# A hybrid decoder layer on one core: another opening, another order of the leading pieces, x transposes a step later, an end by token tile

## The chip, the core and the metric

The kernel runs on one core of one Trainium2 chip. The metric is the device time of one execution in microseconds. TensorE (PE) multiplies; VectorE (DVE), ScalarE (ACT) and GpSimd (POOL) do the rest, and SyncE (SP) issues most of the transfers. All data is float32.

## The reference

One layer for 256 tokens of width 2048, with float32 weights. Every product with a weight matrix is to be done at near float32 precision.

```python
h = x + 0.5 * swiglu(rmsnorm(h, ffn1_norm), w_gu1, w_dn1)     # d_ff 5632
proj = rmsnorm(h, mix_norm) @ w_in                            # u | v | z | x | B | C | dt
gu, gv, z, xbc, dt_raw = split(proj)
a_out = gelu(gu) * (W_s rmsnorm(gelu(gv)) + b)                # causal inside 128 tokens
m_out = rmsnorm((ssd_scan(silu(conv(xbc)), softplus(dt_raw + bias), ...) + D * x) * silu(z))
h = h + concat([a_out, m_out]) @ w_out
h = h + memory_cross_attention(rmsnorm(h, xa_norm), rmsnorm(mem, mem_norm), w_q, w_kv, w_o)
h = h + 0.5 * swiglu(rmsnorm(h, ffn2_norm), w_gu2, w_dn2)
return rmsnorm(h, final_norm)
```

## The kernel before

**The product.** A float32 operand is split into a rounded part `hi` (a cast on ACT, L143) and a remainder `lo` (a subtraction on DVE, L148). A product is three PE matmuls: hi by hi, hi by lo, lo by hi. All matmuls come from line 73 and all transposes from line 76, and PE runs them in program order.

**The feed-forward steps.** Line numbers here are those of before. `ffn` (used twice) works in columns `c` of 512 gates and 512 ups. A column's product over the 2048 rows of the weight is `proj_sum`: eight *units*, one for each *piece* of 256 rows. A unit loads 1 MB of weights into `raw` (three buffers `wraw`), casts (`whigh`, three buffers), subtracts (`wlow`, two buffers) and multiplies. Of kind C it takes 24 matmuls of 128x512; of kind S (a Strassen-like scheme on sums and differences) 21. The string `GU_KINDS = "CSCSCSCC"` gives each piece its kind. The operand made from the normalised input, `xp_ffn`, has one form per piece: PE transposes four 128x128 tiles of `h` (`tpose`), then for a C piece ACT scales each half of the piece, k = 0 and 1 (L299) and DVE takes the remainder (L300); for an S piece ACT writes `forms` (L352), DVE makes differences (L356 to L358), and ACT and DVE split 3 and 4 forms (L360, L361) into a tile of seven forms. The root-mean-square factor is applied at a column's end, so its sums (`sum_sq`, L273) come beside the first units.

**Steps.** After each unit `step()` counts one and runs the jobs that `later(fn, by)` has put off by that many units. A job's PE transposes therefore stand between two units. The order on DVE, ACT and POOL is set by a scheduler, and each engine runs its row of instructions strictly in that order: an instruction that waits holds up those behind it.

**The opening.** `h` is loaded from `x` by 512 columns and token tile, 256 KB each, and the first three weight pieces by blocks of 256 KB between them, all on SP's queue. `FIRST = [0, 2, 4, 1, 6, 3, 5, 7]` is the order of pieces in the first column of the first step. In the second step the first column runs in plain order.

**The mix stage.** `proj_feat` makes the columns B, C and x of the input projection, feature on the partition, four units a column; `conv_silu` (L530 to L534) convolves them and writes `xf` with ACT, and the job `x_tokens` turns `xf` back to tokens (4 transposes and 2 copies, L637) one unit later for the first half of a column and two for the second. `make_dt` (L562) makes the scan's step sizes with four small matmuls. The x columns are followed by V (the gate's other input), and under it run the scan's first DVE steps `xdt`, `y`, `dec` (L659 to L675) and `gate_weights`.

**The end.** In the last column group `finish(n)` is called for each 512 columns of the output after both token tiles: sums of squares, the factor `rstd_f` (POOL, L281), the scaling and eight output transfers, all on SP's queue (L928).

## Time and profile before

| | us |
|---|---|
| three runs, median (2544.72 to 2545.55) | 2544.92 |
| the profiled execution | 2544.5 |
| its span, from the first to the last instruction | 2542.8 |
| PE busy in it | 2491.5 |
| DVE busy | 1822.0 |
| ACT busy | 1233.8 |
| mean granted clock of PE | 0.993 |

The profiled execution is 0.4 us under the median, and 1.7 us of it lie outside of the span. A row of the timeline gives the start of an instruction, counted from the span's start, its length, and in brackets how long its engine had been idle ahead of it and what ended the wait. Matmuls are pipelined, so the difference of two starts is the cost of one, not its length.

### The profile page before, as it was taken

Reading aid. Unit: us, or ns where it says so; the run is one execution under the profiler, and the core shown is the slowest. Engines: PE = TensorE matmul, PEld = TensorE weight load, DVE = VectorE, ACT = ScalarE, POOL = GpSimd, SP = SyncE. Lnnn points to the kernel's source line nnn. Section 1 sums busy time; section 2 is a strip of 40 time slices with the busy share of each in tenths; the row PEclk is TensorE's granted clock in tenths of the full one; section 3 lists DMA queues with packets and bytes.
Section 4 is the critical chain, followed back from the end, with each engine's and each line's share of the span. In section 5 each row is a group of like instructions: output and inputs, shape, how many; then the busy total and the mean of one; then the engine's idle time right before and its main releaser. Section 6 shows DMA issues by size and latency. Waiting matters only on the chain.

```text
span 2542.8 us, 31168 instructions
## 1 busy us (share of the span) xinstructions
PE 2491.5 (98%) x12732; PEld 2126.1 (84%) x12732; DVE 1822.0 (72%) x1644; ACT 1233.8 (49%) x1100; POOL 21.3 (1%) x44
## 2 busy tenths in 40 slices
PE   7999999999999999999999999999999999999998
PEld 5788888888889997888888999988788888888886
DVE  6888779897776657664555555445689877898886
ACT  5455445555545445434544444334555544555443
POOL 0000000000000000000000000000000000000000
PEclk9999999999999999999999999999999999999999
DMA  5565665656654545555555655555556666666664
GB/s 188 185 208 189 198 211 184 204 193 199 199 173 163 183 151 200 184 166 183 196 184 192 206 182 167 165 169 179 182 184 196 199 198 197 201 198 198 199 208 140
DMA packets 197185, 476.74 MB, mean 187 GB/s; under 512 B 14273, under 2 KB 14433, under 8 KB 196273
## 3 DMA queue, kind: packets, MB, share of 16 engines
q1 hardware_dynamic: 195216, 465.88, 56.2%
q0 software_dynamic: 1680, 8.73, 1.0%
q8 instruction: 99, 1.62, 0.3%
q14 instruction: 46, 0.37, 0.0%
q10 hardware_dynamic: 144, 0.13, 0.0%
HBM read 472.57 MB, written 2.13 MB: 187 GB/s over the span
## 4 chain that ended last, share of the span: by engine, by line
PE 90%; DVE 6%; ACT 2%; issue 1%; DMA 1%; SPq 0%; ACTq 0%; DVEq 0%; POOL 0%
PE acc L73 86%; DVE lo L148 3%; PE tpose L76 2%; ACT hi L143 1%; PE yp L73 1%; DMA raw<-in_w_gu 0%; DVE cacc L532 0%; PE logits L73 0%; PE o L73 0%; DVE sum L159 0%; DVE sum L161 0%; PE mixed L73 0%; DVE sum L160 0%; DVE hids L361 0%; PE dt L73 0%
## 5 line engine op out<-in xcount | busy, mean ns | idle before, releaser
L148 DVE TENSOR_TENSOR lo<-raw,hi 128x2048 fp32r<-128x2048 f32 (+1 forms) x440 | 959.5, 2183 | 443.9 <-PE acc L73 360.0
L143 ACT CAST hi<-raw 128x2048 fp32r<-128x2048 f32 (+1 forms) x440 | 805.1, 1830 | 950.5 <-PE acc L73 802.9
L73 PE MATMUL acc<-hi,xp_ffn 128*128 128x512 f32 x1760 | 558.5, 392 | 10.2 <-ACT xp_ffn L299 6.8
L73 PEld LDWEIGHTS acc<-hi,xp_ffn 128*128 128x128 f32 x1760 | 332.5, 189 | 82.9 <-ACT xp_ffn L299 8.7
L73 PE MATMUL acc<-lo,xp_ffn 128*128 128x512 f32 x880 | 344.4, 391 | 1.2 <-DVE lo L148 1.2
L73 PE MATMUL acc<-hi,hid 128*128 128x512 f32 x1088 | 340.4, 390 | 0.0
L148 DVE TENSOR_TENSOR lo<-sum,hi 128x2048 fp32r<-128x2048 f32 x86 | 196.8, 2289 | 117.3 <-ACT hi L143 117.3
L143 ACT CAST hi<-sum 128x2048 fp32r<-128x2048 f32 x86 | 164.4, 1912 | 178.4 <-DVE sum L161 146.7
L73 PE MATMUL acc<-hi,xt_mix 128*128 128x512 f32 x768 | 244.4, 395 | 0.0
L73 PEld LDWEIGHTS acc<-hi,hid 128*128 128x128 f32 x1088 | 204.2, 188 | 42.3
L73 PE MATMUL acc<-lo,hid 128*128 128x512 f32 x544 | 211.7, 389 | 0.0
L73 PEld LDWEIGHTS acc<-lo,xp_ffn 128*128 128x128 f32 x880 | 166.5, 189 | 36.1 <-DVE lo L148 1.7
L73 PE MATMUL acc<-xt_mix,hi 128*128 128x256 f32 x1024 | 188.5, 286 | 0.0
L73 PEld LDWEIGHTS acc<-hi,xt_mix 128*128 128x128 f32 x768 | 145.5, 189 | 30.8 <-issue 0.7
L73 PEld LDWEIGHTS acc<-xt_mix,hi 128*128 128x128 f32 x1024 | 161.9, 194 | 0.3
L73 PE MATMUL acc<-hi,xp_ffn1s 128*128 128x512 f32 x462 | 150.4, 394 | 3.4 <-ACT hi L143 1.8
L73 PE MATMUL acc<-hi,xp_ffn2s 128*128 128x512 f32 x462 | 150.0, 394 | 3.3 <-DVE xp_ffn L300 2.3
L73 PE MATMUL acc<-lo,xt_mix 128*128 128x512 f32 x384 | 150.6, 392 | 0.0
L73 PE MATMUL acc<-xt_mix,lo 128*128 128x256 f32 x512 | 146.3, 286 | 0.7 <-DVE lo L148 0.7
L408 DVE TENSOR_TENSOR part<-acc,part 128x512 f32<-128x512 f32 x208 | 138.2, 684 | 9.3 <-ACT part L427 4.2
L73 PEld LDWEIGHTS acc<-lo,hid 128*128 128x128 f32 x544 | 102.2, 188 | 20.9
L159 DVE TENSOR_TENSOR sum<-raw 128x1024 f32<-128x1024 f32 x86 | 105.0, 1221 | 7.9 <-DMA raw<-in_w_gu 5.5
(246 smaller groups left out, 3284.1 us busy)
## 6 DMA issues: line engine op xcount, KB each, us to landing
raw<-in_w_gu SPq DMA_DIRECT2D x280, 512.0 KB, 3.9
raw<-in_w_in SPq DMA_DIRECT2D x80, 1024.0 KB, 5.2
raw<-in_w_dn SPq DMA_DIRECT2D x68, 1024.0 KB, 5.5
raw<-in_w_gu SPq DMA_DIRECT2D x144, 256.0 KB, 4.1
raw<-in_w_out SPq DMA_DIRECT2D x32, 1024.0 KB, 5.5
raw<-in_w_kv SPq DMA_DIRECT2D x32, 1024.0 KB, 5.3
raw<-in_w_q SPq DMA_DIRECT2D x16, 1024.0 KB, 5.1
raw<-in_w_o SPq DMA_DIRECT2D x16, 1024.0 KB, 5.5
```

The costliest lines, as they stand in the source:

```text
L73: return pe(nc.tensor.matmul(out, lhsT=lhsT, rhs=rhs, start=start, stop=stop))
L76: return pe(nc.tensor.transpose(out=out, in_=in_, identity=identity))
L143: nc.scalar.copy(out=t[:, :n], in_=x[:, :n])
L148: nc.vector.tensor_tensor(out=t[:, :n], in0=x[:, :n], in1=hi[:, :n].bitcast(F32), op=ALU.subtract)
L159: nc.vector.tensor_tensor(out=t[:, 0:2], in0=raw[:, 0:3:2], in1=raw[:, 3:4].broadcast_to([P, 2, NC]), op=ALU.add)
L408: nc.vector.tensor_tensor(out=out, in0=a, in1=b, op=op)
```

## The change

- **Opening.** `x` is loaded by pieces of 256 columns (both token tiles, 256 KB in rows of 1 KB) in the order in which the pieces are used, between the weight pieces 0, 2 and 4. The first weight piece comes in four blocks of 256 KB, is cast and subtracted by blocks of 512 columns (`split(raw, fine)`), and its unit runs all products of k = 0 ahead of those of k = 1. A new `keep_busy` issues six and then four plain float32 matmuls of 128x256 on zeros (its result is not used), around the transposes of the first piece.
- **Order and kinds of the leading units.** In the first column of both steps the order is `[0, 2, 4, 6, 1, 3, 5, 7]` with kinds `CCCCCSCC`; pieces 1 and 3 have S operands and run as C, with plain forms read from the S operand by `FORM`. For this the S operand holds eight forms rather than seven, and both splits are 128x512 wide.
- **Half steps.** A C unit counts half a step after half of its products and half at its end. The transposes of the pieces are put at half steps, and the sums of squares later.
- **`evac`** is called for each token tile and output half as it ends, no longer for both halves at once.
- **`make_dt`**: the four small matmuls run back to back, and the two DVE steps after them.
- **`x_tokens`** one unit later.
- **The second step's opening**: pieces 4, 6, 5 and 7 are put at 1, 1.5, 2.5 and 3 units, the sums of squares at 3.
- **The end**: `finish(n, t)` is called for each token tile as soon as its columns are done, and two of the eight output transfers go by ACT's queue.

```diff
-    def step(shut=False):
-        steps[0] += 1
+    def step(shut=False, of=1):
+        steps[0] += of
...
+        for b in range(2 * KP):
+            nc.scalar.copy(out=hi[:, b], in_=raw[:, b])
+            nc.vector.tensor_tensor(out=lo[:, b], in0=raw[:, b], in1=hi[:, b].bitcast(F32), op=ALU.subtract)
...
+                def tok(t, k):
+                    if len(x.shape) == 4:
+                        return x[:, 0, FORM[t, k]], x[:, 1, FORM[t, k]]
+                    return x[:, k, t * P:(t + 1) * P], x[:, k, S + t * P:S + (t + 1) * P]
+                turns = [((t, j), range(KP)) for t, j in HOME]
+                if m < fine:
+                    turns = [((t, j), (k,)) for k in range(KP) for j in range(2) for t in range(NT)]
...
+                    if a == len(turns) // 2 - 1:
+                        step(shut=s_at[0] <= m < s_at[-1], of=0.5)
+                step(shut=s_at[0] - 1 < m < s_at[-1], of=0.5)
...
+                for i in (2 * n, 2 * n + 1):
+                    later(lambda i=i: self.xts.put(i, srcs, i % 2 * KP, self.c0 + n * KG),
+                          {4: 1, 6: 1.5, 5: 2.5, 7: 3}.get(i, by))
+                later(lambda: self.stats(n), 3)
...
+    FIRST_KINDS, FIRST = "CCCCCSCC", [0, 2, 4, 6, 1, 3, 5, 7]
...
+    keep_busy(6)
+    x_operand(0)
+    keep_busy(4)
+    for i, by in ((2, 0.5), (1, 1.5), (4, 1.5), (6, 2), (3, 2.5), (5, 3), (7, 3.5)):
+        later(lambda i=i: x_operand(i), by=by)
...
-            later(lambda c=c, i0=i0, xf=xf: x_tokens(c, i0, xf), by=1 + i0 // 2)
+            later(lambda c=c, i0=i0, xf=xf: x_tokens(c, i0, xf), by=2 + i0 // 2)
...
+            (nc.scalar if t and m < 2 else nc.sync).dma_start(out=o_v[:, t, m * NC:(m + 1) * NC], in_=o)
```

ACT at the opening, before (`xp_ffn_136` holds pieces 0 and then 2, `hi<-raw` is the cast of a weight piece; the third row of casts is the third piece's):

```order
L143 CAST hi<-raw 128x2048
L299 ACTIVATE xp_ffn_136<-tpose,col 128x256
L352 ACTIVATE forms<-tpose,col 128x256 x2
L360 CAST xp_ffn1s<-forms 128x384
L299 ACTIVATE xp_ffn_136<-tpose,col 128x256
L143 CAST hi<-raw 128x2048
L360 CAST xp_ffn1s<-forms 128x512
L143 CAST hi<-raw 128x2048
L299 ACTIVATE xp_ffn_136<-tpose,col 128x256
L352 ACTIVATE forms<-tpose,col 128x256 x2
```

The same place after (line numbers of after; `xp_ffn_141` holds pieces 0 and 2, `xp_ffn_237` pieces 4 and 6):

```order
L325 ACTIVATE xp_ffn_141<-tpose,col 128x256
L147 CAST hi<-raw 128x2048
L325 ACTIVATE xp_ffn_141<-tpose,col 128x256
L147 CAST hi<-raw 128x2048
L325 ACTIVATE xp_ffn_141<-tpose,col 128x256 x2
L147 CAST hi<-raw 128x2048
L381 ACTIVATE forms<-tpose,col 128x256 x2
L389 CAST xp_ffn1s<-forms 128x512
L325 ACTIVATE xp_ffn_237<-tpose,col 128x256
L147 CAST hi<-raw 128x2048
L389 CAST xp_ffn1s<-forms 128x512
L325 ACTIVATE xp_ffn_237<-tpose,col 128x256 x3
```

Ahead of these rows stands the first weight piece's cast, in four parts of 128x512. The first S operand (`forms`) has moved from the first row but one to behind four weight casts. Between the two halves of piece 0's operand (the first two rows of `xp_ffn`) now stands the cast of the second weight piece, where an S operand's `forms` and its first split stood; behind the first half of piece 4's operand (the first `xp_ffn_237`) now stands the fifth weight piece's cast.

ACT where the first x columns are turned to tokens, before (`xf` is the conv's output, `COPY y` follows the transposes on PE):

```order
L143 CAST hi<-raw 128x2048
L534 ACTIVATE xf<-cacc,col 128x256
L530 ACTIVATE cacc<-hi,col 128x256 x2
L143 CAST hi<-raw 128x2048
L534 ACTIVATE xf<-cacc,col 128x256 x2
L530 ACTIVATE cacc<-hi,col 128x256
L637 COPY y_6334<-tpose 128x256
L637 COPY y_6335<-tpose 128x256
L534 ACTIVATE xf<-cacc,col 128x256
L143 CAST hi<-raw 128x2048
L637 COPY y_6334<-tpose 128x256
```

The same place after:

```order
L147 CAST hi<-raw 128x2048
L596 ACTIVATE xf<-cacc,col 128x256
L592 ACTIVATE cacc<-hi,col 128x256 x2
L147 CAST hi<-raw 128x2048
L596 ACTIVATE xf<-cacc,col 128x256 x2
L592 ACTIVATE cacc<-hi,col 128x256
L596 ACTIVATE xf<-cacc,col 128x256
L147 CAST hi<-raw 128x2048
L700 COPY y_6338<-tpose 128x256
L700 COPY y_6339<-tpose 128x256
L147 CAST hi<-raw 128x2048
L700 COPY y_6338<-tpose 128x256
L700 COPY y_6339<-tpose 128x256
```

The copies of a column's first half now stand behind the whole convolution's `xf` and a weight cast, a unit later than before.

DVE at the end of the program, before (`h_92` and `h_93` are the last two groups of 512 columns, each product adds to them, `rstd_f` is the factor of a token tile):

```order
L405 SCALAR_TENSOR_TENSOR h_92<-acc,h_92 128x512
L405 SCALAR_TENSOR_TENSOR h_93<-acc,h_93 128x512
L917 TENSOR_TENSOR h_92<-h_92,fw 128x512
L405 SCALAR_TENSOR_TENSOR h_92<-acc,h_92 128x512
L405 SCALAR_TENSOR_TENSOR h_93<-acc,h_93 128x512
L917 TENSOR_TENSOR h_92<-h_92,fw 128x512
L279 TENSOR_REDUCE ms<-ss_f 128x1
L280 TENSOR_SCALAR ms<-ms 128x1
L279 TENSOR_REDUCE ms<-ss_f 128x1
L280 TENSOR_SCALAR ms<-ms 128x1
L925 TENSOR_SCALAR h_92<-h_92,rstd_f_18638 128x512
L923 SCALAR_TENSOR_TENSOR h_93<-h_93,rstd_f_18638,fw 128x512
```

The same place after:

```order
L438 SCALAR_TENSOR_TENSOR h_92<-acc,h_92 128x512
L438 SCALAR_TENSOR_TENSOR h_93<-acc,h_93 128x512
L982 TENSOR_TENSOR h_92<-h_92,fw 128x512
L438 SCALAR_TENSOR_TENSOR h_92<-acc,h_92 128x512
L305 TENSOR_REDUCE ms<-ss_f 128x1
L306 TENSOR_SCALAR ms<-ms 128x1
L988 SCALAR_TENSOR_TENSOR h_93<-h_93,rstd_f_18613,fw 128x512
L990 TENSOR_SCALAR h_92<-h_92,rstd_f_18613 128x512
L982 TENSOR_TENSOR h_92<-h_92,fw 128x512
L438 SCALAR_TENSOR_TENSOR h_93<-acc,h_93 128x512
L305 TENSOR_REDUCE ms<-ss_f 128x1
L306 TENSOR_SCALAR ms<-ms 128x1
```

The scaling of the first token tile now stands ahead of the last addition to `h_93` rather than behind it.

## Rows read from the trace of the kernel before

**Rows 1.** The page: busy time of each engine, and the chain that ended last
```profile
PE 2491.5 (98%) x12732; PEld 2126.1 (84%) x12732; DVE 1822.0 (72%) x1644; ACT 1233.8 (49%) x1100; POOL 21.3 (1%) x44
...
PE 90%; DVE 6%; ACT 2%; issue 1%; DMA 1%; SPq 0%; ACTq 0%; DVEq 0%; POOL 0%
```
**Rows 2.** PE's waits: line, releaser, us in total, times, longest
```profile
PE tpose L76 <- ACT xf L534: 10.4, 4, 3.8
PE acc L73 <- DVE xp_ffn L300: 6.9, 5, 2.3
PE acc L73 <- ACT xp_ffn L299: 6.8, 2, 5.3
...
PE dt L73 <- DVE dt L562: 1.6, 1, 1.6
```
**Rows 3.** Timeline of the opening: start, us, engine, line, instruction [idle before <-releaser]
```profile
9.91 1.90 ACT L143 CAST hi<-raw 128x2048 fp32r<-128x2048 f32 x1 [7.17 <-DMA raw<-in_w_gu]
...
11.71 0.47 ACT L299 ACTIVATE xp_ffn<-tpose,col 128x256 fp32r<-128x256 f32 x1
11.84 2.29 DVE L148 TENSOR_TENSOR lo<-raw,hi 128x2048 fp32r<-128x2048 f32 x1 [4.44 <-ACT hi L143]
...
12.24 0.80 PE L73 MATMUL acc<-hi,xp_ffn 128*128 128x512 f32 x1 [5.35 <-ACT xp_ffn L299]
...
18.10 1.92 ACT L143 CAST hi<-raw 128x2048 fp32r<-128x2048 f32 x1 [0.76 <-DMA raw<-in_w_gu]
...
21.45 1.03 PE L76 MATMUL tpose<-ident,h 128*128 128x128 f32 x8
...
44.46 0.48 PE L73 MATMUL acc<-hi,xp_ffn1s 128*128 128x512 f32 x1
...
71.68 0.39 PE L73 MATMUL acc<-hi,xp_ffn 128*128 128x512 f32 x1
...
76.89 0.61 PE L73 MATMUL acc<-hi,xp_ffn 128*128 128x512 f32 x2
```
**Rows 4.** Stretches: us, busy of PE, PEld, DVE, ACT, POOL; PEclk, DMA share, GB/s
```profile
35.20:42.00 6.80, 5.63 (x14) 4.13 (x13) 3.94 (x8) 4.29 (x15) 0.72 (x1) 0.50 0.14 53
...
65.90:69.40 3.50, 3.12 (x7) 2.48 (x8) 3.07 (x5) 0.00 (x0) 0.00 (x0) 0.51 0.77 290
...
782.70:786.10 3.40, 3.40 (x16) 3.37 (x16) 1.43 (x6) 1.82 (x3) 0.00 (x0) 0.50 0.88 279
902.20:905.60 3.40, 3.11 (x15) 3.11 (x16) 3.23 (x4) 1.84 (x6) 0.00 (x0) 0.50 0.15 20
956.80:963.60 6.80, 5.77 (x15) 4.66 (x16) 3.13 (x8) 2.30 (x5) 0.00 (x0) 0.50 0.75 299
1837.40:1840.90 3.50, 3.38 (x8) 2.74 (x9) 0.00 (x0) 0.45 (x1) 0.00 (x0) 0.51 0.85 295
```
**Rows 5.** Timeline: plain float32 matmuls of 128x256, two records each
```profile
1030.72 3.61 PE L73 MATMUL st<-xdt,sum 128*128 128x256 f32 x16
```
**Rows 6.** Timeline of PE where it turns the conv's output (xf)
```profile
876.20 0.55 PE L76 MATMUL tpose<-ident,xf 128*128 128x128 f32 x3 [2.21 <-ACT xf L534]
...
902.49 0.90 PE L76 MATMUL tpose<-ident,xf 128*128 128x128 f32 x3 [2.17 <-ACT xf L534]
...
957.83 0.90 PE L76 MATMUL tpose<-ident,xf 128*128 128x128 f32 x3 [3.84 <-ACT xf L534]
```
**Rows 7.** Timeline of DVE ahead of the scan
```profile
966.14 2.29 DVE L148 TENSOR_TENSOR lo<-raw,hi 128x2048 fp32r<-128x2048 f32 x1 [5.49 <-PE acc L73]
```
**Rows 8.** Timeline of PE at the opening of the second feed-forward step
```profile
1831.43 0.50 PE L73 MATMUL acc<-hi,xp_ffn2s 128*128 128x512 f32 x1 [0.98 <-ACT forms L352]
...
1837.52 0.77 PE L73 MATMUL acc<-hi,xp_ffn2s 128*128 128x512 f32 x1 [2.30 <-DVE xp_ffn L300]
```
**Rows 9.** Timeline of the end
```profile
2530.88 0.69 DVE L405 SCALAR_TENSOR_TENSOR h<-acc,h 128x512 f32<-128x512 f32 x1 [0.67 <-PE acc L73]
...
2533.62 4.49 SPq L928 DMA_DIRECT2D out<-h  x8
```

More of the change, by code (lines that the diff above doesn't have):

```diff
@@ L130, in load @@
             return raw
+        if fine:
+            for (k, j), b in at.items():
+                nc.sync.dma_start(out=raw[:, b, :], in_=rows[k * P:(k + 1) * P, cs[j]:cs[j] + NC])
+            return raw
         for j, c in enumerate(cs):
@@ L133, in load @@
             src = rows[:, c:c + NC]
-            if e > b and not fine:
+            if e > b:
                 nc.sync.dma_start(out=raw[:, b:e + 1:e - b, :], in_=src.rearrange("(k p) n -> p k n", p=P))
@@ L149, in low, with split @@
         return t
-    def split(raw):
-        hi = high(whigh, raw, 2 * KP)
-        return hi, low(wlow, raw, hi, 2 * KP)
+    def split(raw, fine=False):
+        if not fine:
+            hi = high(whigh, raw, 2 * KP)
+            return hi, low(wlow, raw, hi, 2 * KP)
+        hi = whigh.tile([P, 2 * KP, NC], F32R, name="hi")
+        lo = wlow.tile([P, 2 * KP, NC], F32R, name="lo")
+        for b in range(2 * KP):
+            nc.scalar.copy(out=hi[:, b], in_=raw[:, b])
+            nc.vector.tensor_tensor(out=lo[:, b], in0=raw[:, b], in1=hi[:, b].bitcast(F32), op=ALU.subtract)
+        return hi, lo
     def split_sums(raw):
@@ L237, in proj_sum @@
             else:
[L238 removed]
+                hi, lo = split(raw, m < fine)
                 x = xps[i]
[L240 to L245 removed]
+                def tok(t, k):
[5 more added lines that the diff above has]
+                    turns = [((t, j), (k,)) for k in range(KP) for j in range(2) for t in range(NT)]
+                for a, ((t, j), ks) in enumerate(turns):
+                    name = HOME[t, j]
+                    product(name, [(*tok(t, k), hi[:, 2 * k + j], lo[:, 2 * k + j]) for k in ks],
+                            m == (c_at[-1] if name == "c11" else n - 1))
+                    if end and ks[-1] == KP - 1:
+                        evac(t, j, banks[name])
+                    if a == len(turns) // 2 - 1:
+                        step(shut=s_at[0] <= m < s_at[-1], of=0.5)
+                step(shut=s_at[0] - 1 < m < s_at[-1], of=0.5)
+                continue
             step(shut=s_at[0] - 1 < m < s_at[-1])
@@ L323, in hybrid_layer @@
     owed = []
-    class Pieces(list):
+    class Pieces(dict):
         def __init__(self, kinds, name):
@@ L330, in add, with put @@
         def add(self, srcs, q, c0):
-            kind = self.kinds[len(self)]
+            return self.put(len(self), srcs, q, c0)
+        def put(self, at, srcs, q, c0):
+            kind = self.kinds[at]
             if kind == "C":
@@ L411, in hybrid_layer, with ffn @@
     GU_KINDS = "CSCSCSCC"
+    FIRST_KINDS, FIRST = "CCCCCSCC", [0, 2, 4, 6, 1, 3, 5, 7]
     DN_KINDS = {5: ("CCSCCSCCCC", None), 6: ("CCCCSCCSCCSC", [0, 1, 2, 3, 4, 5, 6, 7, 8, 10, 9, 11])}
-    def ffn(nrm, w_gu, w_dn, done, order=None):
+    def ffn(nrm, w_gu, w_dn, done=None, each=None, fine=0):
         for c_from, c_to in ((0, 5), (5, 11)):
@@ L456, in mid, with evac @@
                     axpy(h[n + 1][:, 1, :], 0.5, y)
-                def evac(t, ps):
-                    for j in range(2):
-                        axpy(h[n + j][:, t, :], 0.5, ps[j])
+                def evac(t, j, ps):
+                    axpy(h[n + j][:, t, :], 0.5, ps)
+                    if each is not None and c_to == 11:
+                        each(n + j, t)
                 proj_sum(w_dn, c_from * NC, hts, kinds, (n * NC, (n + 1) * NC), mid, evac, turn)
-                if c_to == 11:
+                if done is not None and c_to == 11:
                     done(n)
@@ L467, in hybrid_layer, with first_load, x_load, x_operand @@
     n1 = Normed("ffn1", C_FFN1, GU_KINDS)
-    FIRST = [0, 2, 4, 1, 6, 3, 5, 7]
-    for n in range(4):
-        for t in range(NT):
-            nc.sync.dma_start(out=h[n][:, t, :], in_=x_v[:, t, n * NC:(n + 1) * NC])
-        if n < 3:
-            ready[id(w_gu1), 0, FIRST[n], (0, DFF)] = load(w_gu1, FIRST[n] * KP * P, (0, DFF), PLAIN, fine=True)
-    def x_operand(n):
-        for q in (0, 2):
-            n1.xts.add([h[n][:, t, :] for t in range(NT)], q, n1.c0 + n * KG)
-    x_operand(0)
-    for n in range(1, 4):
-        later(lambda n=n: x_operand(n), by=n)
-    for n in range(4):
-        later(lambda n=n: n1.stats(n), by=3)
+    nc.sync.dma_start(out=h[0][:, :, :KP * P], in_=x_v[:, :, :KP * P])
+    def first_load(i):
+        ready[id(w_gu1), 0, i, (0, DFF)] = load(w_gu1, i * KP * P, (0, DFF), PLAIN, fine=i == 0)
+    def x_load(i):
+        c = i * KP * P
+        nc.sync.dma_start(out=h[c // NC][:, :, c % NC:c % NC + KP * P], in_=x_v[:, :, c:c + KP * P])
+    first_load(0)
+    x_load(2)
+    first_load(2)
+    for i in (1, 4):
+        x_load(i)
+    first_load(4)
+    for i in (3, 6, 5, 7):
+        x_load(i)
+    def x_operand(i):
+        n, q = i // 2, i % 2 * KP
+        n1.xts.put(i, [h[n][:, t, :] for t in range(NT)], q, n1.c0 + n * KG)
+    idle = const.tile([P, S], F32, name="idle")
+    nc.vector.memset(idle, 0.0)
+    def keep_busy(n):
+        ps = side("idle")
+        for i in range(n):
+            matmul(ps[:, :S], idle[:, :P], idle, start=True, stop=True)
+    keep_busy(6)
[3 more added lines that the diff above has]
+        later(lambda i=i: x_operand(i), by=by)
+    for n in range(4):
+        later(lambda n=n: n1.stats(n), by=4 + n / 2)
     nx = Normed("mix", C_MIX)
-    ffn(n1, w_gu1, w_dn1, nx.chunk, FIRST)
+    ffn(n1, w_gu1, w_dn1, nx.chunk, fine=1)
     misc = wsum.tile([P, 4, NC], F32, name="sum").rearrange("p a n -> p (a n)")
```

78 lines of the change are left out of this document (39 added, 39 removed).

## The prediction

> **What bounds the kernel now.** I read the page first. PE is busy 98% of the span and holds 90% of the chain that ended last; DVE is at 72% and ACT at 49% [rows 1]. The two can be late at a place, but neither bounds the whole. PE's work stays almost the same, so whatever the change gains has to be time in which PE stands still or runs slowly. Those places are found by two views. The waits of PE, by line and releaser, name the engine that was late: transposes of the conv's output waited 10.4 us for ACT in four waits, matmuls of the feed-forward steps waited 6.9 and 6.8 us for the two halves of `xp_ffn`, and the small dt matmuls 1.6 us once [rows 2]. The timeline of the first 77 us says where most of the `xp_ffn` waits lie: the first matmul starts at 12.24 after a wait of 5.35 for ACT, unit 0 ends at 21.45 where it hands over to transposes, the third unit ends at 44.46, and the eighth starts at 71.68 and ends at 77.1 (the last two of its 24 start at 76.89) [rows 3]. Last, the table of stretches shows the second kind of loss: a granted clock of 0.50, that is 1.2 rather than 2.4 GHz, in six stretches, and before each PE had stood still or had run short instructions [rows 4]. A stretch of length L at half clock costs L/2.
>
> The profiled execution took 2544.5 us, the span 2542.8, the median of the runs 2544.92. I sum against 2544.5 and add the 0.4 between at the end. About 0.2%, 5 us, is what a measurement of this kernel can tell from no change.
>
> **Opening.** Unit 7 runs undisturbed: 24 matmuls from 71.68 to 77.1, 0.227 us each [rows 3]. Before, the first column has 5 C units of 24 and 3 S units of 21, 183 matmuls or 41.5 us; the 28 transposes after the first piece's cost 0.13 each (the row at 21.45: 8 in 1.03), 3.6 us. That makes 45 us of work, but from 12.24 to 77.1 there are 65: 20 us are lost.
>
> After, two S units become C, so 189 matmuls, 42.9 us, and with the transposes 46.5. The start: between ACT's first cast at 9.91, which had waited for the fourth block of weights, the sixth of the queue, and its third at 18.10, the eighteenth, 12 blocks of 256 KB landed in 8.19 us, 0.68 each [rows 3]. The first weight piece is now complete with the fifth block, at about 9.2. Three of its four casts lie ahead of that; the last ends at 9.8, the first half of the operand 0.47 later, and PE starts at about 10.2. The 12 matmuls of k = 0 end at 13.2, since the remainder is not long in coming. Here is the first new wait: on ACT the cast of the second weight piece stands ahead of the operand's other half. That piece is now the seventh to tenth block, lands at 12.6, is cast by 14.5 (1.90), the half follows at 15.0, and on DVE its remainder stands behind the second piece's 2.29 of subtraction: 14.5, 16.8, 17.3. PE waits 4.1. The idle matmuls don't matter for this sum: a plain float32 128x256 costs two records of 0.226 [rows 5], ten of them 4.5 us at full clock and 9 at half; even if they push the first product from 10.2 to 12.5, the wait that ends at 17.3 takes most of it up.
>
> The second new wait is in the third unit. The first half of piece 4 is ready at its start, but behind it ACT has the cast of the fifth weight piece, which can begin only when the second unit's end frees a buffer of `whigh` (three). So 1.90 of cast, a forms cast, the other half and its remainder come to about 4 us after the unit's start, where PE wants them at 0.7 to 1.4: I take 2.7. Then 10.2 + 46.5 + 4.1 + 2.7 = 63.5. The clock: before, 6.8 and 3.5 us of the opening ran at half [rows 4], 5.1 us lost. Two waits of 3 to 4 us are left of many, so I take half of that, 2.6: the column ends at 66.1, a gain of **11.0**. Bounds: 14 if the second wait is covered, 6 if both stretches at half clock come back and one more wait as long as the second.
>
> **x transposes, one unit later.** Four waits of 10.4 in all [rows 2], three of which are shown [rows 6]: PE arrives 2.2, 2.2 and 3.8 before ACT has `xf`. The clock then falls for 3.4 us (1.7 lost) and from 957.8 to 963.6 (2.9) [rows 4]; 15.0 in all. A unit in this stage lasts 5.8 (from 876.20 to 902.49 are four, less two waits) [rows 6], more than the longest wait, so the transposes find `xf` ready. What is late next is the scan's start: the last transposes move from the end of the x columns into V's first unit but one, and DVE's chain `xdt`, `y`, `dec` starts later by the same unit. DVE stood idle for 5.49 ahead of it, waiting for PE [rows 7], so most of this is covered; what speaks against full cover is the POOL transfer of `dec`, which in the new order stands behind the `affine_select` of the gate's weights. I take **14.0**, bounds 8 (DVE comes into the first V units late by three of its 2.29 [rows 7]) and 15.3.
>
> **dt.** The wait of 1.6 [rows 2] stood between the two token tiles' small matmuls, because the second waited for DVE to read the first. Back to back it goes, and with it the stretch of 3.4 at half clock right behind it (1.7) [rows 4]. **3.3**; between 1.6, if the clock falls on account of the small matmuls themselves, and 3.5.
>
> **Second opening.** Waits of 0.98 and 2.30 [rows 8], and 3.5 at half clock behind the second (1.75) [rows 4], sum 5.0; six more matmuls cost 1.4. **3.7**, from 0 (another wait in its place as in the first opening's third unit) to 4.
>
> **End.** The last matmul's output is added at 2530.88, and SP issues eight transfers from 2533.62 on over 4.49 us [rows 9]. After, the first tile's transfers are out early, but on DVE the last addition to `h_93` stands behind three operations that wait for the first tile's factor, so it starts at about 33.0 rather than 30.9; then sum, factor and four scalings follow, and the last issue comes at 37.5 against 38. **0.4**, from a loss of 1.2 to a gain of 1.
>
> **The rest.** Wider splits of the S operands and the new place of the mix operand's second half cost no PE time, as ACT has 51% to spare [rows 1]; I enter a **loss of 0.5**, bounds 0 and 2. The order elsewhere is unchanged.
>
> Sum: 11.0 + 14.0 + 3.3 + 3.7 + 0.4 - 0.5 = 31.9. 2544.5 - 31.9 = 2512.6, against the median **2513.0**.
>
> A rule speaks against the opening. The rows give 0.68 us a block of 256 KB, in a queue that holds several at once [rows 3]. The Trainium skill, "DMA: Bandwidth & Descriptors", section "Bandwidth", says to batch transfers to 1 MiB or more to reach 75% of the peak. If each block paid 2.6 us alone, an estimate from that page's fit (section "Anatomy of one DMA") of 2.0 us and a term for the bytes, the tenth block would land at about 26 and the kernel end near 2526. The trace disagrees with this: blocks of this size were queued before and came at 0.68.
>
> **The rivals.**
> 1. *The opening gains little.* The waits on ACT's order are longer than I think, or the clock stays low after them; the idle matmuls run when PE would be waiting anyway. For it: the operand's second half stands behind a cast in two places. Against it: the first five blocks come no later. With a gain of 2 in place of 11 and 2 at the second opening: 2513.0 + 9 + 1.7 = 2523.7.
> 2. *DVE bounds V's first units.* For it: it has 72% of its time taken [rows 1], and a whole unit of slack is spent. Against it: 5.49 idle [rows 7]. x gives 8: 2519.
> 3. *Blocks come slower in the new order,* at twice 0.68: the first five land 3.4 late, the next five 3.4 more, and PE, which waits for both, loses 7 of the opening's 11: 2520. Against it the spacing of 0.68 over 12 blocks of the same size [rows 3].
> 4. *Slower than before.* The wait of the third unit, an operand's half behind a weight cast that needs the previous unit's end, repeats in units 1 to 7 of both first columns. 14 places by 2.7, 38 us, makes 2551. It decides from 2.3 a place on. Against it: in the order, later pieces have their halves together.
> 5. *The change does less than it says at the small places:* dt and the second opening give nothing, as their clock falls for another reason: 2520.
>
> **How the numbers follow.** My sum 0.55, the first rival 0.16, the second 0.12, the third 0.03, the fourth 0.02, the fifth 0.12. The predicted time is my sum's. Low end: 14 + 15.3 + 3.5 + 4 + 1 is 38 and gives 2507; high end: the first rival and the second together, 2530, are unlikely, so it reaches somewhat beyond the first alone, to 2526. That leaves out about 2 in 10. Faster by over 0.2% holds for all but the fourth rival and a mix of all bad bounds: 0.96; same 0.03, slower 0.01.
>
> **What would show it.** In the trace after, PE's first matmul at about 10 to 12, unit 0 ending at 20 or 21 still, the first column's end near 66 rather than 77.1. PE's waits should have no row for transposes on `xf`, none for dt, and a row for `xp_ffn` with two or three waits of 2 to 5 us. The stretches around 780, 900 and 955 should have a clock of 1.00. If V's first units show waits on DVE, the second rival holds. I am wrong at the root if the clock falls where PE does not wait.

## The result, and the profile after

The changed kernel takes 2517.91 us (median of 4 runs, 2517.1 to 2519.19) against 2545.22 (2544.72 to 2545.55): a ratio of 0.9893, interval 0.9876 to 0.991. The gain is 27.3 us. 2513.0 was forecast, with a range of 2506 to 2526. The direction is right and the time lies in the range, but 5 us of the gain are missing, and they are not missing where I looked for them: every part that I costed gave what I had said, to 0.1 us, or more, and the place to which I had given 0.5 us took back 10.

The profiled run took 2519.19, the slowest of the four; its span is 2517.5. The page, busy time and chain, which answer [rows 1]:

```profile
PE 2490.9 (99%) x12764; PEld 2124.5 (84%) x12764; DVE 1806.5 (72%) x1631; ACT 1230.0 (49%) x1100; POOL 19.0 (1%) x44
...
PE 85%; DVE 9%; issue 3%; ACT 2%; DMA 1%; SPq 0%; DVEq 0%; POOLq 0%; POOL 0%; ACTq 0%
```

DVE's share of the chain is now 9%, where it was 6%. PE's waits (line, releaser, us in total, times, longest), which answer [rows 2]:

```profile
PE acc L73 <- DVE lo L152: 5.8, 11, 1.4
PE acc L73 <- ACT xp_ffn L325: 3.4, 3, 1.7
PE acc L73 <- DVE hid L320: 2.2, 6, 0.6
PE acc L73 <- DVE xp_ffn L326: 1.6, 1, 1.6
PE idle L73 <- DVE idle L533: 1.3, 1, 1.3
PE tpose L76 <- DVE part L475: 1.0, 3, 0.5
```

The waits on `xf` and on dt are gone, those on `xp_ffn` are down from 13.7 to 5.0. What leads the list now are small waits for DVE in the columns of the feed-forward steps: `lo` 5.8, `hid` 2.2, `part` 1.0. Before, the waits on `lo` came to as much, but 3.0 of them (at 14.19 and 66.28) lay in the opening:

```profile
PE acc L73 <- DVE lo L148: 5.9, 10, 1.8
```

The opening in the timeline of PE after (it answers [rows 3]):

```profile
9.89 0.50 PE L73 MATMUL acc<-hi,xp_ffn 128*128 128x512 f32 x1 [0.64 <-ACT xp_ffn L325]
...
13.05 0.60 PE L76 MATMUL tpose<-ident,h 128*128 128x128 f32 x4
14.66 0.50 PE L73 MATMUL acc<-hi,xp_ffn 128*128 128x512 f32 x1 [1.01 <-ACT xp_ffn L325]
...
17.00 0.80 PE L73 MATMUL acc<-hi,xp_ffn 128*128 128x512 f32 x2 [1.61 <-DVE xp_ffn L326]
...
30.41 0.50 PE L73 MATMUL acc<-hi,xp_ffn 128*128 128x512 f32 x1 [1.74 <-ACT xp_ffn L325]
```

PE starts at 9.89 (10.2 was forecast), ends the products of k = 0 at 13.05 (13.2), has the second half complete at 17.00 (17.3), and waits once more in the third unit. The first column ends at 65.13 rather than 77.12. The records of the clock begin where it first rises, at 7.29. From there on, in the stretches (us, busy of PE, PEld, DVE, ACT, POOL; granted clock, DMA share, GB/s; they answer [rows 4]), there is half clock behind the two waits and nowhere else until the end:

```profile
17.50:20.90 3.40, 3.40 (x10) 2.66 (x9) 1.04 (x3) 1.84 (x3) 0.00 (x0) 0.50 1.07 373
...
31.20:34.60 3.40, 3.40 (x9) 2.62 (x10) 0.78 (x2) 0.47 (x1) 0.00 (x0) 0.50 0.80 295
...
772.00:776.00 4.00, 4.00 (x34) 3.79 (x34) 2.76 (x4) 2.81 (x4) 0.00 (x0) 1.00 0.03 6
895.00:905.00 10.00, 10.00 (x86) 10.00 (x86) 2.92 (x3) 3.17 (x5) 0.00 (x0) 1.00 0.58 191
940.00:950.00 10.00, 10.00 (x56) 8.51 (x55) 7.22 (x7) 5.92 (x8) 1.73 (x3) 1.00 0.81 298
```

Where the time went, by the two traces (2544.5 and 2519.19). A column's *loss* is the sum, over its matmuls and transposes, of the start-to-start time above the usual one (0.227 us for 128x512, 0.109 for a transpose).

| part | forecast | by the traces |
|---|---|---|
| opening: end of column 0, 77.12 to 65.13 | 11.0 | 12.0 |
| dt: loss around it, 3.50 to 0.28 | 3.3 | 3.2 |
| x transposes | 14.0 | 15.3 |
| second step's column 0, 48.73 to 44.79 | 3.7 | 3.9 |
| end: from the last matmul's start, 12.35 to 11.53 | 0.4 | 0.8 |
| columns 1 to 10 of both steps: losses 3.7 to 13.2 | 0 | -9.5 |
| the rest | -0.5 | -0.6 |
| sum | 31.9 | 25.1 (measured 25.3) |

Columns 1, 2 and 8 hold most of the new losses: in the first step 1.97, 2.30 and 2.08 (before 0.63, 1.09 and 1.07). DVE's rows of column 1 show what it is up against there:

```profile
69.75 2.29 DVE L152 TENSOR_TENSOR lo<-sum,hi 128x2048 fp32r<-128x2048 f32 x1 [0.18 <-ACT hi L147]
71.96 2.28 DVE L152 TENSOR_TENSOR lo<-raw,hi 128x2048 fp32r<-128x2048 f32 x1
...
81.63 2.29 DVE L152 TENSOR_TENSOR lo<-sum,hi 128x2048 fp32r<-128x2048 f32 x1 [2.06 <-ACT hi L147]
...
92.30 2.29 DVE L152 TENSOR_TENSOR lo<-sum,hi 128x2048 fp32r<-128x2048 f32 x1 [2.05 <-ACT hi L147]
```

From one `lo<-sum` to the next, one C and one S unit, it is 10.67 us (81.63 to 92.30). PE needs 45 matmuls, 10.2. DVE is not idle in that time but for 2.05, in which ACT casts the sums that DVE has just made, so this idle time is part of the chain. From the second `lo<-sum` of a column to the third it is 10.67 to 10.69 in every column of both kernels but one, also in those that lose nothing. So the share of 72% on the page hides a stretch in each column in which DVE is slower than PE, and the two C units at the column's end make it up again. What differs is DVE's start: in a column that loses nothing the first `lo<-sum` starts 1.4 to 2.6 us ahead of the column, in column 1 of the first step 4.6 behind it (69.75 against 65.13).

### The profile page after: what moved, and what is told of

The parts are those of the page before. It is cut to its first block, busy times and chain, and to the rows that moved or that the text cites. A ratio compares the mean times of both kernels' runs of the same rounds, so it can differ in the third digit from the quotient of the medians.

```text
span 2517.5 us, 31208 instructions
## 1 busy us (share of the span) xinstructions
PE 2490.9 (99%) x12764; PEld 2124.5 (84%) x12764; DVE 1806.5 (72%) x1631; ACT 1230.0 (49%) x1100; POOL 19.0 (1%) x44
## 4 chain that ended last, share of the span: by engine, by line
PE 85%; DVE 9%; issue 3%; ACT 2%; DMA 1%; SPq 0%; DVEq 0%; POOLq 0%; POOL 0%; ACTq 0%
PE acc L73 81%; DVE lo L152 5%; PE tpose L76 2%; ACT hi L147 2%; DMA raw<-in_w_gu 1%; DVE sum L170 1%; DVE part L441 1%; PE yp L73 1%; DVE sum L171 1%; DVE part L475 0%; PE logits L73 0%; PE o L73 0%; DVE sum L172 0%; DVE cacc L594 0%; DVE hid L320 0%
## 5 line engine op out<-in xcount | busy, mean ns | idle before, releaser
L152 DVE TENSOR_TENSOR lo<-sum,hi 128x2048 fp32r<-128x2048 f32 x82 | 187.7, 2289 | 106.9 <-ACT hi L147 106.9
L147 ACT CAST hi<-sum 128x2048 fp32r<-128x2048 f32 x82 | 156.7, 1911 | 164.9 <-DVE sum L172 158.2
```

The source lines that it names most:

```text
L147: nc.scalar.copy(out=t[:, :n], in_=x[:, :n])
L152: nc.vector.tensor_tensor(out=t[:, :n], in0=x[:, :n], in1=hi[:, :n].bitcast(F32), op=ALU.subtract)
```

## The experiments

Three theories for the missing 5 us: **A**, DVE enters column 1 with too little lead; **B**, the wider splits of S operands; **C**, loads that now and then land late. The table has all runs (us; lost: columns 1 to 10 of the first and of the second step in the profiled run). The kernel before, measured again beside each group of runs, had medians from 2544.4 to 2545.6, so about 1 us between two groups tells nothing:

| kernel | time (lowest to highest) | column 0 ends | lost |
|---|---|---|---|
| before | 2545.2 (2544.7 to 2545.6) | 77.12 | 2.5 + 1.3 |
| changed | 2517.9 (2517.1 to 2519.2) | 65.13 | 7.3 + 5.9 |
| open_old | 2525.5 (2524.8 to 2525.6) | 77.83 | 2.7 + 3.9 |
| ffn2_old | 2518.5 (2517.6 to 2520.3) | 66.52 | 5.9 + 3.0 |
| narrow | 2519.5 (2517.8 to 2520.7) | 62.73 | 7.0 + 6.5 |
| x_old | 2534.9 (2532.5 to 2539.5) | 65.17 | 6.7 + 6.2 |
| less_s | 2526.8 (2524.4 to 2527.0) | 63.65 | 10.7 + 7.6 |
| no_idle | 2513.1 (2512.4 to 2513.6) | 63.79 | 4.2 + 4.1 |
| first_dve024 | 2517.9 (2516.5 to 2518.7) | 61.95 | 7.6 + 7.9 |
| dt_old | 2525.9 (one run) | 65.25 | 7.2 + 7.5 |
| no_idle_pad | 2515.2 (2514.1 to 2516.2) | 63.88 | 6.7 + 4.7 |
| before_pad | 2548.5 (2546.2 to 2549.4) | 77.66 | 4.3 + 1.5 |
| best | 2508.3 (2508.1 to 2508.7) | 59.81 | 4.5 + 3.6 |
| best_s5 | 2504.8 (2504.1 to 2506.7) | 59.49 | 3.6 + 2.1 |

**open_old** puts the opening of before back:

```diff
-    ffn(n1, w_gu1, w_dn1, nx.chunk, fine=1)
+    ffn(n1, w_gu1, w_dn1, nx.chunk, lead=(GU_KINDS, OLD))
...
```

> The changed kernel with the opening of before put back (loads, order and kinds of the first column of the first feed-forward step, no idle matmuls). In the trace of the changed kernel the first column ends at 65.13 rather than 77.12, 12.0 earlier, but columns 1, 2 and 8 of that step lose 1.97, 2.30 and 2.08 us where before they lost 0.63, 1.09 and 1.07. Theory A (DVE carries its backlog): DVE needs 10.67 us for a C and an S unit together and PE 10.2, so DVE enters column 1 with as little lead as PE's waits in column 0 leave it; with the old opening columns 1 and 2 fall back to about 0.6 and 1.1, and the time is about 12 - 2.5 = 9.5 above that of the changed kernel, 2527.4. Rival B (wider splits of the S operands, 0.14 us more on DVE for each): columns 1, 2 and 8 keep their losses, 12 above, 2530. Rival C (loads that land late now and then): the losses move to other columns, 2526 to 2530 with no pattern.

It costs 7.6, not 12: of the 12.7 by which column 0 ends later, 4.6 come back in columns 1 to 10 of the first step. Columns 1 and 2 fall back to 0.63 and 1.17 as theory A said; that columns 8 and 10 fall too, to 1.23 and -0.04 from 2.08 and 0.95, A doesn't explain, nor that columns 6 and 9 of the second step, which the edit doesn't touch, go from 1.28 and 0.55 to nothing. The edit does two things, though: with the opening it takes the ten idle matmuls away, which alone cost 4.8 (no_idle, below). Against no_idle the old opening costs 12.4, to about 1, and there the columns that A doesn't explain are down too (1.12, -0.04, 0.22 and -0.04). What the old opening does to the columns is then almost only column 1, 0.63 against 1.97: 1.3 us.

**ffn2_old** puts the second step's opening back:

```diff
-    ffn(n2, w_gu2, w_dn2, each=finish)
+    ffn(n2, w_gu2, w_dn2, each=finish, lead=(GU_KINDS, None))
...
```

> The changed kernel with the second feed-forward step's opening of before (plain order, pieces and sums of squares where they stood, three S pieces of kinds as before). Its column 0 lost 5.44 before and 0.15 now, with six matmuls more (1.36); columns 1, 2, 6, 8, 9 lost 0.8 in all before and 5.8 in the profile of the changed kernel. Theory A: the lead that DVE had from PE's waits comes back, columns 1 and 2 lose about 0.8 rather than 2.9, so undoing costs 3.9 - 2.1 = 1.8: 2519.7. Rival B: the losses stay, 3.9 above: 2521.8. Rival C: as B in the mean, with losses at other columns than in the changed kernel's profile.

A difference of 0.6, less than the scatter of the runs: column 0 is 3.9 longer again, but column 1 loses -0.04 rather than 1.79, and the trailing columns vary. So this part gains 3.9 at its place and gives 1.8 of it back one column later; what makes up the rest is not shown, as in this profile column 0 of the first step, which the edit doesn't touch, also ends 1.4 later.

**narrow** goes back to seven forms in every S operand but two:

```diff
-            for x, f0, f1 in ((a, 0, 4), (b, 4, 8)):
+            for x, f0, f1 in ((a, 0, 4), (b, 4, 8)) if wide else ((a[:, 1:4], 0, 3), (b, 3, 7)):
...
```

> The changed kernel with seven forms (splits of 3 and 4) in every S operand but the two whose plain forms are read as C pieces. Theory A: DVE saves 0.14 in ten places among 22 columns, no more than 1 us: 2517 to 2518. Rival B: the losses of columns 1, 2 and 8 go back to those of before, 4 to 5 us less: 2513 to 2514. Rival C: no change.

No gain, and columns 1, 2 and 8 lose as much (2.01, 2.25, 2.01): theory B falls. (Column 0 ends 2.4 earlier in this profile, with one stretch at half clock rather than two; the runs' median doesn't show it.)

**x_old** puts the x transposes back:

```diff
-            later(lambda c=c, i0=i0, xf=xf: x_tokens(c, i0, xf), by=2 + i0 // 2)
+            later(lambda c=c, i0=i0, xf=xf: x_tokens(c, i0, xf), by=1 + i0 // 2)
```

> The changed kernel with the transposes of the conv's output where they stood. The prediction's term was 14.0, bounds 8 and 15.3; in the traces the waits on xf are gone and the clock stays at 1.00 there, and from the first of these transposes to the scan's scores the lead of the changed kernel grows from 8.9 at the end of dt to 25.8. All theories: 2532 to 2533; if the scan's start had taken part of the gain, less than 2530.

The wait is back to the digit, as PE's waits show:

```profile
PE tpose L76 <- ACT xf L596: 10.4, 4, 3.8
```

The scan's scores start at 961.80 rather than 946.92, 15.5 later when what the two runs differ by until then is taken off. The scan's start took nothing: rival 2 is out. (Between the medians it is 17.0, with single runs from 2532.5 to 2539.5.)

**less_s** makes the middle S unit of columns 1, 2 and 8 a C unit:

```diff
-                    proj_sum(w_gu, 0, nrm.xts, GU_KINDS, (c * NC, DFF + c * NC), mid, evac)
+                    proj_sum(w_gu, 0, nrm.xts, "CSCCCSCC" if c in (1, 2, 8) else GU_KINDS,
+                             (c * NC, DFF + c * NC), mid, evac)
```

> The changed kernel with one S unit fewer in columns 1, 2 and 8 of both feed-forward steps (the middle one becomes C): three matmuls more in each, 0.68 us, 4.1 in all, and about 4.3 us less work for DVE in each. In the profile of the changed kernel these six columns lose 1.97, 2.30, 2.08, 1.79, 1.15 and 1.02, 10.3 in all. Theory A (DVE's 10.67 us for a C and an S unit sets the pace there): the losses go, all but 1 us, and the time falls by 9.3 - 4.1 = 5.2 to about 2512.7. Rival C (late loads, wherever they fall): the losses stay and the time rises by 4.1 to 2522.

A miss: 8.9 slower. In column 1 of both steps the loss falls, from 1.97 and 1.79 to 0.80 and 0.68, but in columns 2 and 8, which also turn an S piece for the down product, it rises to 5.72, 4.45, 2.84 and 4.39, with this row among PE's waits:

```profile
PE acc L73 <- DVE hid L320: 11.3, 6, 2.6
```

The kinds changed DVE's order around those operands too, so in columns 2 and 8 the run tells nothing on theory A.

**no_idle** takes the ten idle matmuls away, and with them their tile of zeros:

```diff
-    keep_busy(6)
     x_operand(0)
-    keep_busy(4)
```

> The changed kernel without the ten idle matmuls. The prediction held that they don't matter, since the first products of k = 0 are followed by a wait anyway: in the changed kernel's trace those 12 run from 9.89 to 13.05 at 0.26 each, and PE then waits for ACT until 14.66 and for DVE until 17.00. At half clock they take 5.4 and end at 15.3, still ahead of 17.00. That gives 2517.5 to 2519. Rival: the clock has to be earned by busy time, so that without them the matmuls behind 17.00 run at half clock for as long as they did before (until 18.2 at least and after each further wait), 2 to 4 us more: 2520 to 2522.

Neither: it is 4.8 faster. PE's waits in the opening are nearly the same: the one at 14.66 is gone, since the products ahead of it end later, and there is one more at 22.21:

```profile
9.95 0.80 PE L73 MATMUL acc<-hi,xp_ffn 128*128 128x512 f32 x1 [4.12 <-ACT xp_ffn L325]
10.54 0.63 PE L73 MATMUL acc<-lo,xp_ffn 128*128 128x512 f32 x1
10.96 1.06 PE L73 MATMUL acc<-hi,xp_ffn 128*128 128x512 f32 x2
...
13.10 0.40 PE L73 MATMUL acc<-lo,xp_ffn 128*128 128x512 f32 x1
13.33 0.63 PE L73 MATMUL acc<-hi,xp_ffn 128*128 128x512 f32 x2
...
17.04 0.73 PE L73 MATMUL acc<-hi,xp_ffn 128*128 128x512 f32 x2 [1.63 <-DVE xp_ffn L326]
22.21 0.73 PE L73 MATMUL acc<-hi,xp_ffn 128*128 128x512 f32 x2 [1.48 <-DVE xp_ffn L326]
30.61 0.50 PE L73 MATMUL acc<-hi,xp_ffn 128*128 128x512 f32 x1 [1.74 <-ACT xp_ffn L325]
```

A product takes 0.43 (10.54 to 10.96) until 13.1 and 0.23 (13.10 to 13.33) from there on. That is half clock and full clock (in the changed kernel's stretch of 0.50 a product takes 0.43 too), and the table of stretches doesn't show the first of the two: it gives 1.00 ahead of the first record of the clock, which is at 13.08 here. The slow products cost nothing, as PE would have waited until 14.66 for ACT. From 13.08 on the records have no stretch at half clock ahead of the end, and column 0 ends 1.3 earlier. A further 4.9 are saved in columns 1 to 10, far away from the edit. There the DVE row of the last S piece of the second step's column 5 differs, first the changed kernel, then no_idle:

```profile
2157.44 1.23 DVE L170 TENSOR_TENSOR sum<-raw 128x1024 f32<-128x1024 f32 x1 [1.84 <-DMA raw<-in_w_gu]
```

```profile
2151.46 1.23 DVE L170 TENSOR_TENSOR sum<-raw 128x1024 f32<-128x1024 f32 x1 [0.78 <-DMA raw<-in_w_gu]
```

Both kernels issue the last block of this load 29.4 us behind the column's start. It lands 5.70 us later in the changed kernel and 4.64 later in no_idle. The DMA view of 2155.0 to 2157.5 of the changed kernel has a packet of the instruction queue in it; that of 2150.0 to 2152.5 of no_idle has none:

```profile
q1 hardware_dynamic: 272, 0.53, 77.1%
q8 instruction: 1, 0.02, 2.7%
```

```profile
q1 hardware_dynamic: 280, 0.54, 75.8%
```

Instruction packets of 16 KB come about every 128 matmuls and take about 1.0 us each; there are 100 in the changed kernel and 99 without the idle matmuls or before. The effect is not this load's alone: from 100 us on, the changed kernel has 33 transfers of gate and up weights for which such a packet starts 0.5 to 3.5 us behind their issue, and they land after 4.89 us in the median, the other 340 after 4.07. That made a fourth theory, **F**: twenty more records ahead of everything move the places at which these packets meet the loads.

**first_dve024** lets DVE write the rounded operand of pieces 0, 2 and 4 of the first step:

```diff
+            if by_dve:
+                hi = nc.vector.tensor_tensor(out=dst[:, q:q + 2, :S], in0=ps,
+                                             in1=col[:, c0 + of:c0 + of + 2].unsqueeze(2).broadcast_to([P, 2, S]),
+                                             op=ALU.mult)
```

> The changed kernel with the rounded part of the operand of pieces 0, 2 and 4 written by DVE, both halves in one instruction, so that in the scheduler's order no half stands behind a weight cast on ACT. The prediction's step: the waits of the opening (1.01, 1.61 and 1.74 us and the clock after them, first column's end at 65.13) come from the operand's second half standing behind a weight cast. If so the three waits go, unit 1 starts when its own weights are split, at about 17, and the first column ends 2.5 to 4 us earlier, near 61.5; of that columns 1 and 2 may take back up to 1 (theory A). Time 2514 to 2516. Rival (the weights' arrival sets the opening: the tenth block is cast from 12.33 and the third piece from 16.59 on): PE waits for the casts instead, column 0 ends at 64 to 65, no change of time.

Column 0 ends at 61.95, 3.2 earlier, as was expected, but this run alone doesn't show the step. Of the first two waits 0.21 is left; the third stays, as 1.78 and 0.60 for DVE. One of the two stretches at half clock is gone, which is 1.7 of the 3.2, and narrow, where the halves stand as in the changed kernel, also ends 2.4 earlier with one stretch. The clean pair is no_idle and best (below). The time is the same, since columns 1 to 10 lose 15.4 rather than 13.2, and a run's scatter is 2.

**dt_old** puts DVE's step back between the small matmuls:

```diff
-        for t in range(NT):
             nc.vector.scalar_tensor_tensor(out=dt[:, t, :], in0=pdt[:, t, :HEADS], scalar=rstd[:, t:t + 1],
                                            in1=rowb[:, 0, :], op0=ALU.mult, op1=ALU.add)
```

> The changed kernel with the dt matmuls of the second token tile behind DVE's step for the first, as before. The prediction's term is 3.3: a wait of 1.6 and 1.7 for a stretch of 3.4 us at half clock right behind it. If the clock falls because of the wait, both come back, 3.2 to 3.5 us: 2521. If the four small matmuls alone pull the clock down, the changed kernel's trace would show it, and only the wait comes back: 2519.5.

Around dt 5.0 are lost rather than 0.3: the wait (2.0) and a stretch twice as long as before at half clock:

```profile
775.50:782.30 6.80, 6.61 (x30) 6.55 (x31) 3.55 (x15) 1.82 (x3) 0.00 (x0) 0.50 0.49 157
```

So the wait brings the fall of the clock with it. This is a single run: against the profile of the changed kernel (2519.19) it is 6.7 slower, of which 4.7 lie here and 1.5 in the columns (column 8 of the second step 2.77 rather than 1.02).

**no_idle_pad** and **before_pad** test theory F, the first with ten tiny matmuls (20 records) in place of the idle ones, the second with thirteen (26) in the kernel before, all at the start, where PE waits for the first load:

```diff
+    ps = side("idle")
+    for i in range(10):
+        matmul(ps[:, :32], idle[:, :P], idle[:, :32], start=True, stop=True)
     x_operand(0)
```

> The changed kernel without its ten idle matmuls but with ten tiny ones (128x32, the same twenty records of PE) at the start, while PE waits for the first load. Without idle matmuls the time was 2513.1, 4.8 under the changed kernel: 1.3 of it at the end of column 0 (63.79 against 65.13), where no stretch at half clock is left, and 4.9 in columns 1 to 10 of both steps (lost 8.3 rather than 13.2). Theory F: PE's instructions come by DMA, one packet of 16 KB of about 1.0 us for every 128 matmuls with their weight loads (99 to 100 packets on the instruction queue), and a load that shares its DMA engine lands about 1 us late; the twenty records shift the places of the packets, from 9 or 12 us ahead of columns 6, 8 and 10 to 4 to 8. With the records back, at places that don't matter, the column losses come back to about 12 to 13 and the time is 2517 to 2518, though the clock stays up. Rival K (the idle matmuls cost by the clock that rises early and falls again): the column losses stay near 8.3 and the time near 2513.

> The kernel before with thirteen tiny matmuls (26 records) ahead of its first transposes, while PE waits for the first load; nothing else changes. Theory F: the instruction packets fall as in the changed kernel's first step (20 records of idle matmuls and 6 of the added ones there), so columns 2, 6, 8 and 10 of the first step lose 1.1, 0.1 to 0.7, 0.9 and 0.3 to 0.9 more than before and the second step's 6 and 9 about 1 and 0.7 more: 2 to 5 us slower, 2547 to 2550. Rival (the records are without effect, the losses belong to the new opening): the time stays at 2545.

In no_idle_pad column 0 ends as in no_idle (63.88), but columns 2, 6, 8 and 10 of the first step lose 0.6, 0.4, 0.6 and 0.9 more, and column 6 of the second 0.7: 3.1 of the 4.9 are back, and 2.1 us of time (between the two groups of runs the kernel before differs by 0.7). The delayed block of column 5 is back as well, 5.37 us from issue to landing. In before_pad, whose program is otherwise that of before, columns 2, 8 and 10 lose 0.77, 0.36 and 0.66 more, at the places where the changed kernel loses, and it is slower by 3.3 us (ratio 1.0013, interval 1.0004 to 1.0023). Not all of that is the columns' 2.0: its profile is 4.9 slower, and 3.9 of that arise between the two steps, where the clock falls near 880 and 934 rather than near 902, and for longer near 784; the second step's column 0 gives 1.6 back. Both runs also add the small tile that the tiny matmuls read, and no run separates it from the records; for the packets speaks that transfers which meet one land later within one and the same run, in before_pad too (4.65 against 3.86 by the count above). So the place of the packets is shown to cost time in the columns; its size, some 2 to 3 us of the 4.9, is less than I said, and the rest stays open.

**best** joins no_idle and first_dve024:

> No idle matmuls, and the rounded part of the operand of pieces 0, 2 and 4 on DVE, as in the run before that did this. There the first column ended at 61.95, 3.2 earlier than in the changed kernel, as was expected, but columns 1 to 10 lost 15.4 rather than 13.2 and nothing was left. Theory F (that was the place of the instruction packets): with the packets where they lie without idle matmuls the columns lose 8 to 9, and the time is 2513.1 less what column 0 still gains, 1 to 2: 2511 to 2512. Theory A alone (DVE's lead is short in columns 1 and 2 whatever comes first): the gain of column 0 is given back there, 2513.

2508.3, another 4.8 less than no_idle and below what either theory gave: column 0 ends at 59.81, 4.0 earlier, and the columns lose 8.1. PE has no wait left in the opening behind the one for its first product, this row of its waits:

```profile
PE acc L73 <- DVE xp_ffn L324: 5.2, 1, 5.2
```

The products up to 16.28 still step at 0.43, as the clock first rises at 16.41; from there on it doesn't fall until the end. The two kernels differ only in who writes the rounded halves, so the waits of 1.63, 1.48 and 1.74 in no_idle came from a half behind a weight cast on ACT.

**best_s5** exchanges two pieces of the first column in both steps:

```diff
-    FIRST_KINDS, FIRST = "CCCCCSCC", [0, 2, 4, 6, 1, 3, 5, 7]
+    FIRST_KINDS, FIRST = "CCCCCSCC", [0, 2, 4, 6, 1, 5, 3, 7]
...
-    for i, by in ((2, 0.5), (1, 1.5), (4, 1.5), (6, 2), (3, 2.5), (5, 3), (7, 3.5)):
+    for i, by in ((2, 0.5), (1, 1.5), (4, 1.5), (6, 2), (5, 2.5), (3, 3), (7, 3.5)):
```

> As the run without idle matmuls and with the rounded parts of pieces 0, 2 and 4 on DVE (2508.3), with pieces 5 and 3 exchanged in the first column of both steps, so that the only S piece, and with it DVE's four additions for the shared products, comes two units ahead of the column's end as in all other columns, no longer one. In every kernel with the changed order, column 1 lost 1.97 in the first step and 1.75 to 1.79 in the second, whatever came before it; with the old opening 0.63, with the plain order -0.04. Theory A in its sharper form (DVE enters column 1 late because those additions, the column's end and the next S piece's sums fall together): both losses go to 0.0 to 0.3, 3 us less: 2505. Rival (DVE's lead is short since PE no longer waits in column 0): the losses stay and the time is 2508.

Column 1 loses 0.62 and -0.04 where it lost 1.97 and 1.79 in best, and the time is 2504.8, 3.5 less (0.9842 of the kernel before, interval 0.9826 to 0.9858). DVE's rows at the start of column 1 (59.81 in best, 59.49 in best_s5), first best:

```profile
61.84 1.75 DVE L152 TENSOR_TENSOR lo<-raw,hi 128x1536 fp32r<-128x1536 f32 x1
63.51 0.75 DVE L480 SCALAR_TENSOR_TENSOR part<-part,rstd_ffn 128x512 f32<-128x512 f32 x1
64.43 2.29 DVE L152 TENSOR_TENSOR lo<-sum,hi 128x2048 fp32r<-128x2048 f32 x1 [0.17 <-ACT hi L147]
```

then best_s5:

```profile
58.56 2.28 DVE L152 TENSOR_TENSOR lo<-sum,hi 128x2048 fp32r<-128x2048 f32 x1
60.76 0.74 DVE L480 SCALAR_TENSOR_TENSOR part<-part,rstd_ffn 128x512 f32<-128x512 f32 x1
...
62.62 1.75 DVE L152 TENSOR_TENSOR lo<-raw,hi 128x1536 fp32r<-128x1536 f32 x1
```

The remainder of the first S unit's sums starts 4.6 us after the column in best and 0.9 ahead of it in best_s5. So the place of the last S piece makes DVE late, and moving it is enough to take the loss away. It is not all that differs from the kernel before, however: in the first step's old order, too, the last S piece (piece 5) is the last unit but one, and there the same remainder starts 3.25 after the column (77.12), with a loss of 0.63:

```profile
80.37 2.28 DVE L148 TENSOR_TENSOR lo<-sum,hi 128x2048 fp32r<-128x2048 f32 x1
```

The other 1.4 us of lateness, and the 1.3 of loss that go with it, came with the new opening (open_old has 3.22 and 0.63). In the new opening PE no longer waits at the column's end, as it did before at 63.95 and 66.28 for 1.83 each; that this is the reason, as theory A first had it, is likely but not shown. In the second step the plain order had the S piece two units ahead, and there the new order alone made the loss: that column 0 loses 0.15 in best_s5 as in best, and column 1 -0.04 rather than 1.79.

## Why the prediction was right, and where it was not

- **The views.** Reading the gain from PE's waits and half-clock stretches was right: the four places gave 34.4 where 32.0 was forecast for them.
- **Opening.** The steps came within 0.3 at three marks (start, end of k = 0, second half complete). But the sum was 1 short by errors both ways, so that it came so close is in part luck. The first wait was entered with 4.1, the whole time from 13.2 to 17.3; PE waited 2.6 of it (1.01 and 1.61) and did four transposes and two products in the rest, which the sum counts again as work. The second wait was 1.7 rather than 2.7, and the clock cost 3.4 (two stretches of 3.4 at half) rather than 2.6. The reading of the clock before was short as well: its records begin at 18.14, and the products ahead of that step at 0.43, so the opening had more than 5.1 us of half clock's cost. That the waits come from a half behind a weight cast is shown by no_idle and best.
- **"The idle matmuls don't matter for this sum"** held up to 17.00, where PE goes on within 0.05 of the same time with and without them, and failed behind it. They cost: 4.8 us less without them, of which 1.3 are in column 0. I had asked only whether they delay PE, not what happens to the clock when PE waits after them, nor what twenty more records do to the rest of the program.
- **x transposes.** 14.0 forecast, 15.3 to 15.5 measured: no wait for DVE took the gain's place, so the upper bound was the right value. (A unit there lasts 6.0 rather than the 5.8 that I read, as only one of the waits lies between the two rows; it changes nothing.)
- **dt, end.** 3.3 against 3.2; 0.4 against 0.8. The end's order is the one that I read, and the first tile's transfers are issued from 1.5 us behind the last matmul's start on, before from 3.2 [rows 9].
- **Second opening.** 3.9 at its place as forecast, but 1.8 of that returns in column 1.
- **"The order elsewhere is unchanged", and a loss of 0.5 for the rest.** This is the step that failed, by 9.5 us in the profile. The order on PE in columns 1 to 10 was indeed the same, and on DVE and ACT nearly so (one split is 512 wide rather than 384, and an addition or a scaling has moved at a column's start). I took from it that their time was the same, and from DVE's 72% [rows 1] that it has slack. The rows of a column would have shown 10.67 against 10.2 for a pair of units. Of the loss, column 1 accounts for 3.2 (it goes with another order of the first column, best_s5; 1.3 of it also with the old opening, open_old), the place of the instruction packets for some 2 to 3 (no_idle_pad, before_pad); the remaining 3 to 4 are not explained, and in single runs they vary by 2.
- **Rivals.** Rival 1 had a low gain of the opening for its cause, but its 2523.7 is not what happened; rivals 2 to 4 did not occur, and of the fifth one half may hold in another way: the second opening is worth 0.6 by the runs, within their scatter, and it is column 1 that takes 1.8 of its 3.9 back, not its clock. On the blocks of 256 KB the trace goes with the rows [rows 3]: the second weight piece, complete with the tenth block, was cast from 12.33 on where I said 12.6. The rule in the Trainium skill, "DMA: Bandwidth & Descriptors", section "Bandwidth", to batch transfers to 1 MiB or more, was not needed for blocks in a queue: 0.68 us for 256 KB is 385 GB/s. The page's figures, those of the estimate of 2.6 us too, are for single transfers that GpSimd issued; these were SP's.

## What to carry to other kernels

A mean share hides a short stretch in which the second engine is the slower one: before counting a gain on the first engine as whole, take one period of the loop that follows and compare both engines' times in it. Where an order is written out by hand, look at what the last piece before a boundary puts on the other engines, since it is paid one stage later. Filler work is to be measured without it, also when it stands where the engine would wait.

## What the runs showed of the hardware

Instruction fetch is visible in the times. Packets of 16 KB on an instruction queue take about 1.0 us each, and there is one for about 128 matmuls with their weight loads (100 for 12764 in the changed kernel). Transfers of weights that such a packet meets landed 0.8 us later than others (4.89 against 4.07 in the median, in the changed kernel). And 26 records that do nothing, in a place where PE waits, made the kernel before 3.3 us slower (1.0004 to 1.0023 of its time), though not all of it in places where loads were late.

With waits of the same length (1.6 and 1.7), the granted clock fell to 0.50 twice in the opening with the idle matmuls ahead, where it had risen at 7.29, and not once without them, where it rose at 13.08; why it does so no run here tells. With the idle matmuls it also fell only once, in narrow and in first_dve024. Until it first rises, products of 128x512 step at 0.43 rather than 0.23, though the profile has no record of the clock for that time: the steps in the timeline show it.
